# SwiGLU gate and up products in seven half-width block products instead of eight

## The chip, the cores and the metric

The kernel runs on one core of a Trainium2 chip. The metric is device time in microseconds (us), the median of several runs; lower is better. Times of the trace come from one profiled execution. TensorE is called PE, its weight loads PEld, VectorE DVE, ScalarE ACT, GpSimd POOL and SyncE SP.

## The reference, cut to what matters

Four residual layers work on 512 tokens of width 1024, all in float32. Each layer is a token mixer and a SwiGLU feed-forward (FFN); the mixers are attention, a gated MLP, a state-space mixer and attention again. The change is in the FFN, which occurs four times:

```python
FFN_HIDDEN = 2816                                  # 22 tiles of 128 columns, 11 pairs of tiles
def rmsnorm(x, g):
    y = x * lax.rsqrt(jnp.mean(x * x, axis=-1, keepdims=True) + EPS)
    return y * g
def swiglu(h, w_gu, w_down):                       # h: 512 x 1024, w_gu: 1024 x 5632, w_down: 2816 x 1024
    gu = h @ w_gu
    return (jax.nn.silu(gu[..., :FFN_HIDDEN]) * gu[..., FFN_HIDDEN:]) @ w_down
x = x + m                                          # m: the mixer
x = x + swiglu(rmsnorm(x, ffn_norm[i]), ffn_w_gu[i], ffn_w_down[i])
```

## The kernel before, in words

Activations stand feature-major: a tile is 128 features by 512 tokens, so x is eight tiles. Each float32 operand of a product is split into a hi part (rounded to the fp32r type, one pass on PE) and a lo part (the rest); a product is then three matmuls, hi by hi, hi by lo and lo by hi (`mm3`). The stationary operand of a matmul is a 128x128 block of weights, the moving one 512 tokens.

Weights come from memory in `raw` tiles of 1 MB (128 x 2048 numbers), two buffers of them (`RAWB`). A class `Stream` brings them in the order in which they are used. Each raw tile is cut into two pieces of 1024 columns; `to_hi` writes the hi part (`whi`) on ACT or DVE, `to_lo` the lo part (`wlo`) by a subtraction on DVE or POOL. Three pieces may stand ready or in use (`WB`).

An FFN (`ffn`) goes through 12 hidden tiles and then through 10. For every pair of hidden tiles it multiplies the gate columns (`fm`, 48 matmuls of 512 tokens into two PSUM banks), then the up columns in the same way. The gate's bank is scaled by the reciprocal norm (`rstdB`) on DVE, goes through Silu on ACT, and is scaled again on DVE; the up bank is multiplied by it and split into hi and lo. When all pairs of the part are done, `outp` multiplies them with the rows of `w_down` and `residual` adds the bank to x.

The order of work on PE, ACT, DVE and POOL is written out at build time by a class `Order`. It keeps a clock of its own with a cost for each kind of instruction, and chooses by it where an instruction goes that could run on two engines (`pick` for hi parts, `better_g` for lo parts and sums) and when it is issued. Its costs count a DVE instruction with both inputs in SBUF and a POOL instruction as excluding each other. On the chip each engine then goes through its list in that order and waits on semaphores.

Of the kernel before, what the change touches and what calls it, by code (L numbers as in the profile page):

```python
# [17 lines left out]
F32 = mybir.dt.float32  # L21
F32R = mybir.dt.float32r
AF = mybir.ActivationFunctionType
ALU = mybir.AluOpType
# [41 lines left out]
class Parts:  # L66


    def __init__(self):
        self.hi = self.lo = None  # L70
        self.ready = Task()


class Order:
# [230 lines left out]
class Stream:  # L305


    def __init__(self, k):
        self.k, self.o = k, k.o
        self.raws, self.pieces = [], []  # L310
        self.next_raw = self.next_piece = 0
        self.done_raw = 0
        self.slack = 0.0

    def add(self, srcs, cuts, side=False):


        raw = {"srcs": srcs, "left": len(cuts)}
        self.raws.append(raw)
        out = []  # L320
        for c in cuts:
            p = {"raw": raw, "cut": c, "n": len(self.pieces), "task": Task(), "side": side}
            self.pieces.append(p)
            out.append(p)
        return out

    def dma(self, dst, srcs, n):

# [4 lines left out]
        return Task(self.o.book("D", 0.00143 * n) + 2.0)  # L333

    def load(self):
        while self.next_raw < min(len(self.raws), self.done_raw + RAWB):
            r = self.raws[self.next_raw]
            self.next_raw += 1
            a, b = r["srcs"][0].shape[1], sum(q.shape[2] for q in r["srcs"])
            t = self.k.wp.tile([P, 2048], F32, tag="raw", name="raw", bufs=RAWB)  # L340
            r["ap"] = t[:, :a * b].rearrange("p (a b) -> p a b", b=b)
            r["task"] = self.dma(r["ap"], r["srcs"], a * b)

    def first(self):

        r = self.raws[0]
        self.next_raw = 1
        t = self.k.wp.tile([P, 2048], F32, tag="raw", name="raw", bufs=RAWB)
        r["ap"] = t.rearrange("p (a b) -> p a b", b=256)
        for n, p in enumerate(self.pieces[:2]):  # L350
            ks = slice(4 * n, 4 * n + 4)
            p["loaded"] = self.dma(r["ap"][:, ks, :], [q[:, ks, :] for q in r["srcs"]], 1024)
            yield

    def issue(self):
        if self.next_piece >= len(self.pieces):
            return
        p = self.pieces[self.next_piece]
        self.next_piece += 1
        self.load()  # L360
        self.o.spawn(self._split(p))

    def _split(self, p):
        nc, o, r = self.k.nc, self.o, p["raw"]
        yield p.get("loaded") or r["task"]
# [3 lines left out]
        lo = self.k.wp.tile([P, 1024], F32R, tag="wlo", name="wlo", bufs=WB)  # L369
        if p["side"]:  # L370
# [8 lines left out]
        r["left"] -= 1  # L379
        if not r["left"]:  # L380
            self.done_raw += 1
            self.load()
        o.finish(p["task"])

    def release(self, p):

        def later():
            yield self.o.clk
            self.issue()
        self.o.spawn(later())  # L390


class Trunk:
    def __init__(self, ctx, tc, io):
        self.tc, self.nc, self.io = tc, tc.nc, io
        self.o = Order()
        pool = lambda **k: ctx.enter_context(tc.tile_pool(**k))


        self.tiny = pool(name="tiny", bufs=1)  # L400
        self.const = pool(name="const", bufs=1)
# [8 lines left out]
        self.stream = Stream(self)  # L410


    def bank_cond(self, kind="ps", n=1):
# [100 lines left out]
    def setup(self):  # L514
# [13 lines left out]
        with self.tc.tile_pool(name="xin", bufs=1, reuse_waits="tile") as pool:  # L528
# [4 lines left out]
            for q in range(4):  # L533
# [3 lines left out]
                xtok.append(v)  # L537
                if q % 2 == 1:
                    next(first)
            for _ in range(WB):  # L540
                self.stream.issue()
            self.sb_consts(pool)
            o.until(lambda: 4.5)
            ps = self.bank()
# [95 lines left out]
        self.x_ready, self.acc_ready = [Task() for _ in range(KT)], Task()  # L640
        self.last_sq, self.n_sq = None, 0

    def residual(self, d, ps, last, kind, next_sub):

        nc, o = self.nc, self.o
        nc.vector.tensor_tensor(self.xT[d], self.xT[d], ps, op=ALU.add)  # L646
        yield o.V(S)
        self.give(kind)
# [71 lines left out]

        return self.stream.add(srcs, [(0, 4, 0, 256), (4, 8, 0, 256)])

    def fm(self, pieces, evac, kind="ps"):

        yield self.bank_cond(kind, 2)
        banks = [self.bank(kind) for _ in range(2)]
        for n, p in enumerate(pieces):
            for qs, i in self.steps():
# [6 lines left out]
                if k == KT - 1:  # L735
                    self.o.spawn(evac(i, banks[i]))
            self.stream.release(p)

    def steps(self):

# [58 lines left out]
    def outp(self, reg, ys, last, kind="ps"):  # L799

        nk, next_sub = len(ys), self.next_sub
        if last:
# [1 line left out]
        for cg, chunks in enumerate(reg):  # L804
            banks = [None] * 4
            for a, b, pieces in chunks:
                d = -1
                for p in pieces:
                    for i in range((p["cut"][3] - p["cut"][2]) // P):
# [9 lines left out]
                            self.mm3(banks[d], (p["h"][:, k - a, c], p["l"][:, k - a, c]),  # L819
                                     (ys[k].hi, ys[k].lo), k == 0, k == nk - 1)  # L820
                        if b == nk:
                            self.o.spawn(self.residual(cg * 4 + d, banks[d], last, kind, next_sub))
                    self.stream.release(p)


    def reg_ffn(self, l):
        wgu = self.io["ffn_w_gu"][l].rearrange("(k p) f -> p k f", p=P)
        wd = self.io["ffn_w_down"][l].rearrange("(f p) d -> p f d", p=P)
        parts, f0 = [], 0
        for nf in (12, 10):  # L830
            gu = []
            for f in range(f0, f0 + nf, 2):
                gu.append([self.reg_in([wgu[:, :, b + f * P:b + (f + 2) * P]]) for b in (0, HID)])
            parts.append((nf, gu, self.reg_out(wd[:, f0:f0 + nf, :])))
            f0 += nf
        return parts

    def ffn(self, l, parts):
        nc, o = self.nc, self.o
        with self.tc.tile_pool(name=f"ffn{l}", bufs=3, reuse_waits="tile") as pool:  # L840
            self.stats(pool)
            for half, (nf, gu, down) in enumerate(parts):
                ys = []
                for g_pieces, u_pieces in gu:
                    gates, two = [None, None], [Parts(), Parts()]
                    n0 = len(ys)
                    ys += two

                    def gate(i, ps, gates=gates):
                        gates[i] = pool.tile([P, S], F32, tag="g", name="g", bufs=4)  # L850
                        yield self.rstdB_ready
                        nc.vector.tensor_tensor(gates[i], ps, self.rstdB, op=ALU.mult)
                        yield o.V(S)
                        self.give()
                        nc.scalar.activation(gates[i], gates[i], AF.Silu)
                        yield o.A(S, tab="silu")
                        yield self.either(gates[i], gates[i], self.rstdB, ALU.mult, S)

                    tasks = {}

                    def gate_(i, ps, tasks=tasks, gate=gate):
                        tasks[i] = o.spawn(gate(i, ps))
                        return
                        yield

                    def up(i, ps, tasks=tasks, gates=gates, two=two, n0=n0):
                        yield tasks[i]
                        a = pool.tile([P, S], F32, tag="a", name="a")
                        nc.vector.tensor_tensor(a, ps, gates[i], op=ALU.mult)
                        yield o.V(S)  # L870
                        self.give()
                        yield from self.parts(two[i], pool, f"a{n0 + i}", a)
                    o.run(self.fm(g_pieces, gate_))
                    o.run(self.fm(u_pieces, up))
                o.run(self.outp(down, ys, half == 1))


    def reg_gm(self, j):
# [911 lines left out]
```

## Time and profile before

| what | value |
|---|---|
| time, median of 3 runs (lowest to highest) | 2779.15 us (2777.06 to 2781.51) |
| time of the profiled execution | 2776.99 us |
| its span, first to last instruction | 2775.1 us |
| PE busy | 2746.3 us, 99% of the span |
| DVE, ACT, POOL busy | 64%, 33%, 19% |
| mean granted clock of TensorE | 0.999 of full speed |

The busy share of PE is a union of matmuls that overlap as they pass through the array: a matmul of 512 tokens is shown 390 ns long, but the next one starts 227 ns after it. So the price of a matmul is read from the distance of starts, or from a run's time divided by its count, not from its own duration. The same holds in a small way for DVE and ACT, whose instructions overlap their neighbours by about 0.1 us.

### The profile page before, as it was taken

Reading aid. Unit: us, or ns where it says so; the run is one execution under the profiler, and the core shown is the slowest. Engines: PE = TensorE matmul, PEld = TensorE weight load, DVE = VectorE, ACT = ScalarE, POOL = GpSimd, SP = SyncE. Lnnn points to the kernel's source line nnn. Section 1 sums busy time; section 2 is a strip of 40 time slices with the busy share of each in tenths; the row PEclk is TensorE's granted clock in tenths of the full one; section 3 lists DMA queues with packets and bytes.
Section 4 is the critical chain, followed back from the end, with each engine's and each line's share of the span. In section 5 each row is a group of like instructions: output and inputs, shape, how many; then the busy total and the mean of one; then the engine's idle time right before and its main releaser. Section 6 shows DMA issues by size and latency. Waiting matters only on the chain.

```text
span 2775.1 us, 34968 instructions
## 1 busy us (share of the span) xinstructions
PE 2746.3 (99%) x14339; PEld 2357.7 (85%) x14339; DVE 1766.5 (64%) x2505; ACT 928.4 (33%) x1532; POOL 522.3 (19%) x397
## 2 busy tenths in 40 slices
PE   8999999999999999999999999999999999999999
PEld 8998788888888888888898898888889999788887
DVE  7887854555465655455887787754555887865453
ACT  4876410113222211112553353310113786511111
POOL 4665400002011100001311011200004656400000
PEclk9999999999999999999999999999999999999999
DMA  4110232234333222323222222223222111222322
GB/s 138 49 61 31 91 105 93 92 98 125 99 99 95 92 91 93 105 88 97 77 76 76 77 77 77 91 91 104 94 90 94 62 48 53 81 94 91 103 91 80
DMA packets 207967, 240.72 MB, mean 87 GB/s; under 512 B 6448, under 2 KB 170416, under 8 KB 207808
## 3 DMA queue, kind: packets, MB, share of 16 engines
q1 hardware_dynamic: 207552, 238.36, 27.2%
q8 instruction: 112, 1.84, 0.3%
q14 instruction: 47, 0.39, 0.0%
q0 software_dynamic: 160, 0.11, 0.0%
q10 hardware_dynamic: 96, 0.03, 0.0%
HBM read 236.38 MB, written 2.10 MB: 86 GB/s over the span
## 4 chain that ended last, share of the span: by engine, by line
PE 95%; DVE 2%; POOL 1%; issue 1%; ACT 1%; DMA 0%; ACTq 0%; SPq 0%; POOLq 0%; DVEq 0%
PE ps L458 85%; PE z L458 4%; PE c L458 3%; PE t L458 1%; DVE xl L616 1%; PE c L472 1%; PE t L472 0%; DMA ws<-in_gm_w_s 0%; DVE x L646 0%; POOL r L502 0%; POOL wlo L502 0%; ACT whi L479 0%; DVE sp_r L1043 0%; DMA rows<-in_ffn_norm 0%; DVE wlo L500 0%
## 5 line engine op out<-in xcount | busy, mean ns | idle before, releaser
L458 PE MATMUL ps<-xh,whi 128*128 128x512 f32 x1792 | 701.9, 392 | 0.0
L458 PE MATMUL ps<-xl,whi 128*128 128x512 f32 x1792 | 698.6, 390 | 2.7 <-DVE xl L616 2.5
L458 PE MATMUL ps<-xh,wlo 128*128 128x512 f32 x1792 | 697.7, 389 | 0.0
L479 ACT CAST whi<-raw 128x1024 fp32r<-128x1024 f32 (+2 forms) x245 | 239.2, 977 | 933.9 <-PE ps L458 881.3
L500 DVE TENSOR_TENSOR wlo<-raw,whi 128x1024 fp32r<-128x1024 f32 (+2 forms) x371 | 450.5, 1214 | 120.3 <-ACT whi L479 103.3
L481 DVE CAST whi<-raw 128x1024 fp32r<-128x1024 f32 (+1 forms) x224 | 155.2, 693 | 415.6 <-PE ps L458 414.7
L458 PEld LDWEIGHTS ps<-xl,whi 128*128 128x128 f32 x1792 | 336.4, 188 | 77.0 <-DVE xl L616 7.0
L458 PEld LDWEIGHTS ps<-xh,whi 128*128 128x128 f32 x1792 | 336.4, 188 | 70.1 <-issue 1.0
L458 PEld LDWEIGHTS ps<-xh,wlo 128*128 128x128 f32 x1792 | 336.3, 188 | 70.1
L458 PE MATMUL ps<-lo,whi 128*128 128x512 f32 x960 | 373.9, 389 | 1.7 <-POOL lo L502 1.7
L458 PE MATMUL ps<-hi,whi 128*128 128x512 f32 x960 | 375.5, 391 | 0.0
L458 PE MATMUL ps<-hi,wlo 128*128 128x512 f32 x960 | 373.7, 389 | 0.0
L458 PE MATMUL ps<-whi,xh 128*128 128x256 f32 (+1 forms) x1152 | 342.9, 298 | 0.0
L458 PE MATMUL ps<-wlo,xh 128*128 128x256 f32 (+1 forms) x1152 | 339.4, 295 | 0.9 <-DVE wlo L500 0.9
L458 PE MATMUL ps<-whi,xl 128*128 128x256 f32 (+1 forms) x1152 | 339.6, 295 | 0.4 <-DVE xl L616 0.3
L502 POOL TENSOR_TENSOR wlo<-raw,whi 128x1024 fp32r<-128x1024 f32 (+1 forms) x97 | 202.3, 2087 | 301.6 <-ACT whi L479 198.8
L502 POOL TENSOR_TENSOR acc<-acc,sq 128x512 f32<-128x512 f32 x31 | 48.5, 1564 | 1041.8 <-ACT sq L630 1040.9
L458 PEld LDWEIGHTS ps<-wlo,xh 128*128 128x128 f32 x1152 | 220.1, 191 | 7.3 <-DVE wlo L500 1.1
L458 PEld LDWEIGHTS ps<-whi,xh 128*128 128x128 f32 x1152 | 219.9, 191 | 6.7 <-issue 0.4
L458 PEld LDWEIGHTS ps<-whi,xl 128*128 128x128 f32 x1152 | 220.0, 191 | 5.8 <-DVE xl L616 0.8
L458 PEld LDWEIGHTS ps<-lo,whi 128*128 128x128 f32 x960 | 180.3, 188 | 39.0 <-POOL lo L502 2.3
L458 PEld LDWEIGHTS ps<-hi,wlo 128*128 128x128 f32 x960 | 180.2, 188 | 37.8
(227 smaller groups left out, 3374.7 us busy)
## 6 DMA issues: line engine op xcount, KB each, us to landing
raw<-in_ffn_w_gu SPq DMA_DIRECT2D x88, 1024.0 KB, 5.1
raw<-in_ffn_w_down SPq DMA_DIRECT2D x32, 1024.0 KB, 5.1
raw<-in_sb_w_qkv SPq DMA_DIRECT2D x23, 1024.0 KB, 5.1
raw<-in_gm_w_in SPq DMA_DIRECT2D x16, 1024.0 KB, 5.4
raw<-in_ssm_w_in SPq DMA_DIRECT2D x16, 1024.0 KB, 5.5
raw<-in_ffn_w_down SPq DMA_DIRECT2D x16, 768.0 KB, 4.5
raw<-in_gm_w_out SPq DMA_DIRECT2D x8, 1024.0 KB, 5.1
raw<-in_ssm_w_in SPq DMA_DIRECT2D x16, 512.0 KB, 5.3
```

What stands on the lines that cost most here:

```text
L458: self.nc.tensor.matmul(out, lhsT=lhsT, rhs=rhs, start=start, stop=stop, skip_group_check=True)
L472: self.nc.tensor.transpose(out, in_, self.ident[:in_.shape[0], :in_.shape[0]])
L479: self.nc.scalar.copy(h, src)
L481: self.nc.vector.tensor_copy(h, src)
L500: self.nc.vector.tensor_tensor(out, a, b, op=op)
L502: self.nc.gpsimd.tensor_tensor(out, a, b, op=op)
L616: nc.vector.scalar_tensor_tensor(out=self.xl[d], in0=x, scalar=gcol(d), in1=self.xh[d].bitcast(F32), op0=ALU.mult, op1=ALU.subtract)
```

## The change

In each FFN the first two pairs of hidden tiles stay as they were ("plain"). For the other nine pairs, the gate columns (128 features x 8 blocks by 256 columns) and the up columns are each taken as a 2 by 2 matrix of blocks: the two hidden tiles by the even and odd blocks of features. The activations are a 2 by 2 matrix too, even and odd blocks by the two halves of the tokens. A 2 by 2 block product has eight block products; here it is written with seven (Strassen's scheme, in Winograd's form). The four weight blocks A11, A12, A21, A22 and the sums S1 = A21 + A22, S2 = S1 - A11, S3 = A11 - A21, S4 = A12 - S2 give the seven weight factors; `halves_in` makes four sums of the activations once per FFN (`th`, `tl`). One product of a factor is 4 blocks x 3 matmuls = 12 matmuls of 256 tokens (`product`). "Unit" below means the gate or the up columns of one pair: seven products, 84 matmuls. The results are put together in SBUF: three banks' contents are copied out by ACT or DVE (`saved`) and three are added by DVE (`added`), one quarter is read straight from its bank.

Each weight factor is split into hi and lo like a piece (512 numbers per partition each): hi on ACT, lo on DVE or POOL. Five of the seven factors go through a ring of six slots (`whi` and `wlo` now both hold whole factors), the factors A22 and S4, used late, through two slots `wt`. A third raw buffer (`more`) is used in the FFN.

The FFN is cut into parts of 8, 8 and 6 hidden tiles, where it was 12 and 10. That makes three sections of units per FFN: 4 units (after the two plain pairs), 8 units and 6 units, each followed by its rows of `w_down`. In the first two parts the second scaling by `rstdB` goes from the gate to `residual`, which then scales the bank (`rx`) and adds it in a second instruction.

```diff
-        for nf in (12, 10):
+        for nf in (8, 8, 6):
             gu = []
             for f in range(f0, f0 + nf, 2):
-                gu.append([self.reg_in([wgu[:, :, b + f * P:b + (f + 2) * P]]) for b in (0, HID)])
+                cols = [wgu[:, :, b + f * P:b + (f + 2) * P] for b in (0, HID)]
+                gu.append([self.reg_in([c]) if f < 4 else self.reg_fast(c) for c in cols])
...
+    def _sums(self, r):                                        # in Stream: the four weight sums of a raw tile
+        o, fast = self.o, r["fast"]
+        yield r["task"]
+        A = {(i, j): r["ap"][:, j - 1::2, (i - 1) * P:i * P] for i in (1, 2) for j in (1, 2)}
...
+        def put(name, dst, a, b, op):
+            yield self.k.either(dst, a, b, op, 512)
...
+        yield from put("S1", s1, A[2, 1], A[2, 2], ALU.add)
...
+        yield from put("S2", s2, s1, A[1, 1], ALU.subtract)
+        yield from put("S3", A[2, 1], A[1, 1], A[2, 1], ALU.subtract)
+        yield fast["A12"]["task"]
+        yield from put("S4", A[1, 2], A[1, 2], s2, ALU.subtract)
...
+    def _factor(self, p, before, placed, tail=False):          # hi and lo of one factor
...
+        yield self.k.to_hi(h, p["src"], 512)
+        yield self.k.to_lo(l, p["src"], h, 512, self.slack)
...
     def to_hi(self, h, src, n, even=True):
         o = self.o
-        if o.pick(A=0.00083 * n + 0.1, V=(0.00052 if even else 0.00104) * n + 0.07) == "A":
+        late = 0.0 if self.fpool is None else 1.5
+        if o.pick(A=0.00083 * n + 0.1, V=(0.00052 if even else 0.00104) * n + 0.07 + late) == "A":
...
+    def product(self, u, name, bank, start):
+        p = u.p[name]
+        for k in range(4):
+            x, w = self.factor_x(name, k), (p["h"][:, k, :], p["l"][:, k, :])
+            for n, (a, b) in enumerate(((0, 0), (0, 1), (1, 0))):
+                self.nc.tensor.matmul(bank[:, :S // 2], lhsT=w[a], rhs=x[b], start=start and k == 0 and n == 0,
+                                      stop=False, skip_group_check=True)
+                self.o.pe(0.1207)
+        self.stream.release(p)
+
+    def fast(self, units):
...
+        for u in units:
...
+            self.product(u, "A11", u.X, True)
+            u.t = u.make()
+            o.spawn(saved(u.t[0][:, :H], u.X, u.s1))
...
+            self.product(u, "A12", u.Y, True)
+            o.spawn(added(u.t[0][:, :H], u.Y, u.s1, u.c11, True))
+            o.spawn(u.rest())
+            if prev is not None:
+                yield from p4(prev)                            # product A22 of the unit before, into its X
+            yield o.due(u.p["S2"]["task"], u.s1)
+            self.product(u, "S2", u.X, False)
+            o.spawn(saved(u.t[0][:, H:], u.X, u.s2))
+            if prev is not None:
+                yield from p3(prev)                            # product S4 of the unit before, into its Z
...
+            self.product(u, "S1", u.Z, True)
+            yield o.due(u.p["S3"]["task"], u.s2)
+            self.product(u, "S3", u.X, False)
+            o.spawn(saved(u.t[1][:, H:], u.X, u.s3))
+            o.spawn(added(u.t[1][:, H:], u.Z, u.s3, u.c22, False))
+            prev = u
...
-    def residual(self, d, ps, last, kind, next_sub):
+    def residual(self, d, ps, last, kind, next_sub, by):
...
+            t = self.fpool.tile([P, S], F32, tag="a", name="rx", bufs=4)
+            nc.vector.tensor_tensor(t, ps, by, op=ALU.mult)
+            yield o.V(S)
+            self.give(kind)
+            yield self.either(self.xT[d], self.xT[d], t, ALU.add, S)
```

On PE, in the first FFN, where the third pair's gate columns begin, the list of before has these rows (`xh`, `xl` are hi and lo of an activation tile, `whi`, `wlo` those of a weight piece, the last number the tokens):

```order
L458 MATMUL ps<-xh_91,wlo 128x512
L458 MATMUL ps<-xh_84,whi 128x512
L458 MATMUL ps<-xl_92,whi 128x512
L458 MATMUL ps<-xh_84,wlo 128x512
L458 MATMUL ps<-xh_85,whi 128x512
L458 MATMUL ps<-xl_93,whi 128x512
```

The list of the changed kernel at the same place, from the end of product A12 to the begin of product S2 (`wlo` here holds hi and lo of one factor, `whi` those of the next; `th`, `tl` are hi and lo of a sum of activations):

```order
L906 MATMUL ps<-xh_91,wlo 128x256
L906 MATMUL ps<-xl_99,wlo 128x256
L906 MATMUL ps<-xh_91,wlo 128x256
L906 MATMUL ps<-th_3944,whi 128x256
L906 MATMUL ps<-tl_3945,whi 128x256
L906 MATMUL ps<-th_3944,whi 128x256
L906 MATMUL ps<-th_4031,whi 128x256
```

The matmuls are half as wide, and every one has a weight load of its own, as before.

On DVE, at the third pair, the list of before has one gate pair and its neighbours like this:

```order
L852 TENSOR_TENSOR g<-ps,rstdB 128x512
L500 TENSOR_TENSOR wlo<-raw,whi 128x1024
L500 TENSOR_TENSOR g<-g,rstdB 128x512
L481 CAST whi<-raw 128x1024
L500 TENSOR_TENSOR wlo<-raw,whi 128x1024
L869 TENSOR_TENSOR a<-ps,g 128x512
L481 CAST hi<-a 128x512
L500 TENSOR_TENSOR lo<-a,hi 128x512
```

The list of the changed kernel at its first units (`sum`, `raw<-raw`, `raw<-raw,sum` are weight sums, `whi<-raw,whi` and `wlo<-raw,wlo` lo parts of factors):

```order
L603 TENSOR_TENSOR whi<-raw,whi 128x512
L929 TENSOR_TENSOR g<-ps,g 128x256
L603 TENSOR_TENSOR raw<-raw,sum 128x4x128
L603 TENSOR_TENSOR whi<-sum,whi 128x512
L603 TENSOR_TENSOR sum<-raw 128x512
L603 TENSOR_TENSOR wlo<-raw,wlo 128x512
L603 TENSOR_TENSOR sum<-sum,raw 128x512
L929 TENSOR_TENSOR g<-ps,g 128x256
L603 TENSOR_TENSOR raw<-raw 128x4x128
L603 TENSOR_TENSOR g<-g,rstdB 128x256
```

The hi casts are gone from DVE to ACT, the instructions are more and shorter, and most of them read two operands in SBUF. On POOL the list of before has, from the norm of the first FFN on to the begin of the next layer, these rows (`acc` belongs to the next norm, `ws` to the next layer):

```order
L502 TENSOR_TENSOR wlo<-raw,whi 128x1024
L502 TENSOR_TENSOR lo<-a,hi 128x512
L502 TENSOR_TENSOR acc<-acc,sq 128x512 x5
L502 TENSOR_TENSOR wlo<-raw,whi 128x1024
L902 AFFINE_SELECT ws<-ws 128x512 x4
```

The list of the changed kernel, at its first units:

```order
L605 TENSOR_TENSOR whi<-raw,whi 128x512
L605 TENSOR_TENSOR whi<-sum,whi 128x512
L605 TENSOR_TENSOR wt<-raw,wt 128x512
L605 TENSOR_TENSOR sum<-more 128x512
L605 TENSOR_TENSOR more<-more 128x4x128
L605 TENSOR_TENSOR wlo<-sum,wlo 128x512
```

POOL, which had hardly anything to do in an FFN, now has about a third of the sums and lo parts of its sections.

## Rows read from the trace of the kernel before

**Rows 1.** The page: span and busy time of the engines.
```profile
span 2775.1 us, 34968 instructions
PE 2746.3 (99%) x14339; PEld 2357.7 (85%) x14339; DVE 1766.5 (64%) x2505; ACT 928.4 (33%) x1532; POOL 522.3 (19%) x397
```
**Rows 2.** Chain of waits, stretches of FFN 1, 3, 4: start, length, what, matmuls.
```profile
314.40 347.20 PE ps L458 x1532
...
1743.13 371.26 PE ps L458 x1640
...
2415.23 320.18 PE ps L458 x1413
```
**Rows 3.** Engines' busy time in FFN 1 and FFN 4, and the four FFNs' sum.
```profile
322.00:666.00 344.00, 344.00 (x1517) 284.44 (x1518) 183.90 (x229) 55.52 (x71) 14.14 (x8) 1.00 0.30 95
...
2423.00:2769.00 346.00, 346.00 (x1537) 286.03 (x1537) 174.02 (x220) 50.57 (x63) 6.02 (x3) 1.00 0.29 92
sum 1391.00, PE 1391.00 PEld 1150.15 DVE 729.32 ACT 216.95 POOL 42.40; mean PE 347.75 PEld 287.54 DVE 182.33 ACT 54.24 POOL 10.60
```
**Rows 4.** Chain of waits, early runs of 256-wide matmuls (first attention).
```profile
29.02 20.20 PE ps L458 x168
...
50.09 5.75 PE ps L458 x48
```
**Rows 5.** Groups by line and shape: busy, mean ns of one, idle before.
```profile
L458 PE MATMUL ps<-whi,xh 128*128 128x256 f32 x1024 | 292.6, 286 | 0.0
L500 DVE TENSOR_TENSOR lo<-a,hi 128x512 fp32r<-128x512 f32 x86 | 63.0, 733 | 5.5 <-ACT hi L479 2.8
L1338 DVE TENSOR_TENSOR yo<-c,eac 128x256 f32<-128x256 f32 x24 | 8.8, 414 | 0.0
L479 ACT CAST r<-s 128x512 fp32r<-128x512 f32 x76 | 47.0, 620 | 5.8 <-DVE s L1626 4.3
L1620 ACT ACTIVATE s<-z 128x256 f32<-128x256 f32 x32 | 12.2, 382 | 0.0
L502 POOL TENSOR_TENSOR r<-s,r 128x512 fp32r<-128x512 f32 x52 | 69.5, 1337 | 84.7 <-ACT r L479 39.2 <-DVE r L481 32.2 <-PE ps L458 13.1
```
**Rows 6.** Timeline, instructions back to back: DVE, then POOL.
```profile
290.20 2.48 DVE L646 TENSOR_TENSOR x<-x,ps 128x512 f32<-128x512 f32 x4
...
147.10 1.29 POOL L502 TENSOR_TENSOR r<-s,r 128x512 fp32r<-128x512 f32 x1 [5.72 <-DVE r L481]
148.36 1.29 POOL L502 TENSOR_TENSOR wlo<-raw,whi 128x512 fp32r<-128x512 f32 x1
```
**Rows 7.** Timeline of FFN 1, DVE and POOL at the same time.
```profile
335.03 2.40 POOL L502 TENSOR_TENSOR wlo<-raw,whi 128x1024 fp32r<-128x1024 f32 x1 [10.73 <-ACT whi L479]
335.51 2.47 DVE L500 TENSOR_TENSOR lo<-a,hi 128x512 fp32r<-128x512 f32 x1 [1.39 <-ACT hi L479]
337.38 1.74 POOL L502 TENSOR_TENSOR lo<-a,hi 128x512 fp32r<-128x512 f32 x1
337.90 0.68 DVE L852 TENSOR_TENSOR g<-ps,rstdB 128x512 f32<-128x512 f32 x1
```
**Rows 8.** Engines' busy time in the first attention, columns as in rows 3.
```profile
85.00:300.00 215.00, 210.08 (x1421) 194.75 (x1421) 172.47 (x264) 157.06 (x311) 123.16 (x85) 0.98 0.16 53
```
**Rows 9.** The page, DMA issues: KB each, us to landing.
```profile
raw<-in_ffn_w_gu SPq DMA_DIRECT2D x88, 1024.0 KB, 5.1
```

More of the change, by code (lines that the diff above doesn't have):

```diff
@@ L325, in add, with add_fast @@
         return out
+    def add_fast(self, src):
+        raw = {"srcs": [src], "left": 7, "tag": ("more", "raw", "raw")[self.n_fast % 3], "loaded": Task(), "fast": {}}
+        self.n_fast += 1
+        self.raws.append(raw)
+        for name in ("A11", "A12", "S2", "S1", "S3", "A22", "S4"):
+            p = raw["fast"][name] = {"raw": raw, "task": Task(), "name": name, "slots": 1, "ready": Task()}
+            (self.tails if name in ("A22", "S4") else self.pieces).append(p)
+        return raw["fast"]
     def dma(self, dst, srcs, n):
@@ new lines, in issue, with _place, _done @@
+        while self.next_tail < len(self.tails) and self.tail_credit and self.k.fpool is not None:
+            p = self.tails[self.next_tail]
+            self.next_tail += 1
+            self.tail_credit -= 1
+            self.o.spawn(self._factor(p, *self._place(1), True))
+    def _place(self, ring):
+        before, self.placed[ring] = self.placed[ring], Task()
+        return before, self.placed[ring]
+    def _done(self, p):
+        r = p["raw"]
+        r["left"] -= 1
+        if not r["left"]:
+            self.flying[r["tag"]] -= 1
+            self.load()
+        self.o.finish(p["task"])
@@ L364, in _split @@
+    def _split(self, p, before, placed):
         nc, o, r = self.k.nc, self.o, p["raw"]
-        yield p.get("loaded") or r["task"]
+        yield r["loaded"]
+        yield [p.get("half") or r["task"], before]
         a0, a1, b0, b1 = p["cut"]
@@ L378, in _split @@
         p["h"], p["l"] = h, l
[L379 to L383, printed above, removed]
+        self._done(p)
     def release(self, p):
@@ L388, in later @@
             yield self.o.clk
+            if p.get("name") in ("A22", "S4"):
+                self.tail_credit += 1
+            else:
+                self.credit += p["slots"]
             self.issue()
@@ L539, in setup @@
                     next(first)
-            for _ in range(WB):
-                self.stream.issue()
+            self.stream.issue()
             self.sb_consts(pool)
@@ L797, in reg_out, with outp @@
                  for a, b in cuts] for c in (0, 512)]
-    def outp(self, reg, ys, last, kind="ps"):
+    def outp(self, reg, ys, last, kind="ps", between=(), by=None):
         nk, next_sub = len(ys), self.next_sub
@@ L821, in outp @@
                         if b == nk:
-                            self.o.spawn(self.residual(cg * 4 + d, banks[d], last, kind, next_sub))
+                            self.o.spawn(self.residual(cg * 4 + d, banks[d], last, kind, next_sub, by))
                     self.stream.release(p)
+                    yield from between
+                    between = ()
     def reg_ffn(self, l):
@@ L839, in ffn @@
         nc, o = self.nc, self.o
+        H = S // 2
+        gcol = self.gain(("ffn", l, l))
         with self.tc.tile_pool(name=f"ffn{l}", bufs=3, reuse_waits="tile") as pool:
+            self.fpool = pool
             self.stats(pool)
[L842 to L853, printed above, removed]
-                        self.give()
[L855 to L862, printed above, removed]
@@ L863, in gate_ @@
                         return
                         yield
[L866 to L873, printed above, removed]
@@ L874, in ffn, with gated @@
-                    o.run(self.fm(u_pieces, up))
-                o.run(self.outp(down, ys, half == 1))
+                    return gen
+                def gated(i):
+                    yield from silu(g.t[i], n)
+                    o.finish(done[i])
+                r = self.rstdB_ready
+                g.quarter = quarter(g, lambda: self.rstdB, r)
+                g.rest = rest(g, lambda i: self.rstdB, [r, r], gated)
+                u = Unit(u_pieces)
+                u.make = lambda: [new_a(), new_a()]
@@ new lines, in units, with gu_steps @@
+                u.quarter = quarter(u, lambda: g.t[1], done[1])
+                u.rest = rest(u, lambda i: g.t[i], done, lambda i: self.parts(two[i], pool, f"a{n0 + i}", u.t[i]))
+                return [g, u]
+            for n, (nf, gu, down) in enumerate(parts):
+                ys, todo, left = [], [], []
+                for g_pieces, u_pieces in gu:
+                    two = [Parts(), Parts()]
+                    if n == 0 and len(ys) < 4:
+                        plain(g_pieces, u_pieces, two, n, len(ys))
+                    else:
+                        todo += units(g_pieces, u_pieces, two, n, len(ys))
+                    ys += two
+                def gu_steps():
+                    left.append((yield from self.fast(todo)))
+                o.run(gu_steps())
+                last = n == len(parts) - 1
+                o.run(self.outp(down, ys, last, between=left[0], by=None if last else self.rstdB))
@@ L878, in reg_gm @@
+        self.fpool = None
     def reg_gm(self, j):
```

223 lines of the change are left out of this document (204 added, 19 removed).

## The prediction

> **What bounds the kernel now.** I read the page first: PE is busy for 2746.3 of 2775.1 us, no other engine above 64% [rows 1]. That alone says little, since matmuls overlap in the records, so the chain of waits came next. In the FFNs it is a single run of PE: 347.20 us with 1532 matmuls without a step between, and the like in the other FFNs [rows 2]. The table by stretches gives the neighbours: over the four FFNs' 1391 us PE is busy all the time at the full clock (1.00), DVE for 729 us (52%), ACT for 217, POOL for 42 [rows 3]. So an FFN costs exactly what its matmuls cost, and whatever takes PE time out is gained as long as the other three keep PE fed. The question is whether they do, as DVE, ACT and POOL get the work for it.
>
> **PE's part.** A 512-wide matmul costs 347.20 / 1532 = 0.2266 us [rows 2]. The trace also has long runs of 256-wide ones of the same kind (fp32r, a full 128x128 weight load for each, 1024 per group [rows 5]): 20.20 / 168 = 0.1202 us and 5.75 / 48 = 0.1198 us [rows 4]. So half the width costs 53%, not 50%: some 13 ns of each matmul do not shrink. A unit (gate or up columns of a pair) was 48 matmuls of 512: 48 x 0.2266 = 10.88 us. It becomes 84 of 256: 84 x 0.120 = 10.08 us. The gain is 0.80 us a unit, 7% where seven products for eight would be 12.5%. There are 4 FFNs x 9 pairs x 2 = 72 units: 72 x 0.80 = 57.4 us (55.9 with the one price, 58.7 with the other). The products with the rows of w_down, and the plain pairs, keep their matmuls.
>
> By the Trainium skill, "TensorE: Matmul & The Clock Gate", Back-to-back issue gap, starts are N/2.4 + 2.5 ns apart, 216 ns and 109 ns. With that the sum would be 3456 x 0.216 - 6048 x 0.109 = 87 us, an estimate from that page. The rows have both widths and give 227 and 120, so the sum goes by the rows.
>
> **What is added beside PE.** I take the 8-unit section of an FFN, 80.6 us of PE, and count in the order what stands on the engines between its first and last 256-wide product. DVE: 62 instructions of 512 columns (or a little less) with both inputs in SBUF, 31 that read a PSUM bank, mostly 256 wide. POOL: 37 of 512. ACT: 66 from SBUF, mostly casts of 512, and 24 copies of 256 from PSUM.
> ACT: 66 x 0.62 + 24 x 0.38 = 50 us of 80.6 [rows 5]. It has room; hi parts come in time, and the casts that left DVE fit there.
> DVE: a row of 512 reads 0.69 to 0.73 us, but four in a row take 2.48 us, with 0.68 for the last: (2.48 - 0.68) / 3 = 0.60 us each [rows 5, 6]. The same for POOL: the second starts 1.26 us after the first [rows 6], 1.34 is the mean of the records [rows 5]. By themselves: DVE 62 x 0.60 + 31 x 0.41 = 50 us, POOL 37 x 1.26 = 47 us. Each fits into 80.6 us.
> They do not run freely beside each other, though. The POOL instruction at 335.03 lasts to 337.43; a DVE subtraction of two SBUF operands issued at 335.51 shows 2.47 us and ends 0.55 us after POOL's end, so it stood still for POOL. The next POOL instruction, at 337.38, needs 1.74 us in place of 1.29, as it waits for that DVE one. The DVE instruction at 337.90 reads a bank, and takes its usual 0.68 us beside POOL [rows 7]. So I add the two kinds that exclude each other: 62 x 0.60 + 37 x 1.26 = 83.8 us against 80.6 of PE. Those on PSUM banks go beside POOL. In the 6-unit section (46 and 31, 60.5 us of PE) it is 66.7; in the 4-unit one (35 and 11) 34.9 against 40.3.
> The Trainium skill, "SBUF — State Buffer", Who interferes with whom, has it as an exclusive lock of a port pair for the whole instruction, for a DVE instruction with two SBUF inputs against a POOL one that reads SBUF, and none for one with at most one SBUF input; the trace agrees with 2.47 and 0.68 us. It is the rule that speaks against this change.
>
> So the two sections run over by 3.2 and 6.2 us. What hides this is the stock: in the order a factor's lo part mostly stands six products ahead of its use, 72 x 0.120 = 8.6 us, and the stock is filled anew while w_down's products run (192 or 144 matmuls of 512, 43.5 or 32.6 us, with 25 DVE instructions and few on POOL). If the instructions cost their recorded lengths instead, the excess is 62 x 0.69 + 37 x 1.34 - 80.6 = 11.8 us and, likewise, 12.8 us, so 3.2 + 4.2 us of PE waits in an FFN, 30 us in four. Bounds of this unknown are 0 and 30 us. I take 4 us, near the lower end, since the pitch of neighbours is what a saturated engine shows; 1 us for each FFN at the end of its 6-unit section, where the order leaves least (a lo part stands 1.8 to 3.7 us ahead).
> A new wait is that of product S2 on the copy of its bank: within the first unit of a section only product A12 (1.44 us) lies between, and ACT's copy of 0.38 us stands behind at most a cast of 0.62 us. With semaphores that is about even: 0 to 0.3 us, 12 sections, I take 2 us. From the second unit on two products lie between, 2.9 us. Behind a late DVE addition, on DVE, stand lo parts that have the same stock.
> Hidden altogether: the sums of the activations (on DVE 12 instructions of 256 columns and 8 of 512 per FFN, some 11 us) beside the plain pairs' 43.5 us of PE, where DVE was half idle; 24 residuals in place of 16 and their second instruction, beside w_down's products; the DMAs, the same bytes, with 5.1 us to land [rows 9] against 10 us a unit and three buffers. Without that cover each would cost what it takes: the residuals, for one, 0.6 to 0.7 us apiece.
>
> **Sum.** Against the profiled execution, 2776.99 us (1.9 over its span): 2776.99 - 57.4 + 4 + 2 = 2725.6. That execution lies 2.2 us under the median of the runs, so 2727.8, called 2728.
>
> **Rivals.**
> Vector-limited sections, still a gain. For it: DVE and POOL together are over PE's time in two of three sections. Against: the stock, and the first attention, where DVE is at 172 and POOL at 123 of 215 us, more than the 70% and 60% here, while PE stays busy for 210 [rows 8]. By the recorded lengths 30 us come back: 2779 - 57 + 30 = 2752; up to 2774.
> Slower. The mechanism: DVE and POOL in single file, those on PSUM banks too, since DVE goes through its list in order and an addition that waits for its product holds up the lo parts behind it. Per unit (62 x 0.69 + 37 x 1.34 + 31 x 0.41) / 8 = 13.1 us against 10.08: 3.06 x 72 = 220 us, less 8.6 us of stock in each of 12 sections = 103: 117 back for 57 gained, 2839 us. It decides from 10.08 + (57 + 103) / 72 = 12.3 us per unit on. For it: the count above is 10.5 us with nothing else. Against: rows 7 (the bank-reader at full speed) and rows 8.
> No change: the waits come to about the 57 us, 2779. It needs 12.3 us a unit just so.
> PE's narrow matmuls cheaper than the early runs show: starts 109 and 216 ns apart would give 2779 - 87 + 6 = 2698. Against: every 256-wide run of the trace.
>
> **How the numbers follow.** Forecast (2718 to 2740) 0.70; vector-limited with a gain 0.14; no change 0.06; slower 0.08; cheaper matmuls 0.02. So faster 0.70 + 0.14 + 0.02 = 0.86, same 0.06, slower 0.08, with 0.2% (5.6 us) as about what a measurement of this kernel can tell from no change. The range goes from 2717 (58.7 us gained, no wait, 3 us of spread of the runs) to 2752 (30 us of waits).
>
> **What would show it.** Right: the 256-wide products start 0.120 us apart in stretches without waits; an FFN's PE run gets 14 us shorter; DVE at about 70% and POOL at 60% in the 8-unit sections; PE's idle time in an FFN a microsecond or two, at the last units of the 6-unit section. Wrong: PE waits for lo parts (DVE or POOL) in the middle of the 8-unit sections, or for the copies of ACT in every unit; a start distance other than 0.120; DVE instructions of 512 with two SBUF inputs at a mean well over 0.9 us.

## The result, and the profile after

The changed kernel takes 2729.53 us (2728.78 to 2734.62, 4 runs); the kernel before took 2778.57 us (2777.06 to 2781.51, 4 runs) beside it. The ratio is 0.9823, with a 95% interval of 0.9808 to 0.9839: 49 us faster. The prediction was 2728, with a range from 2717 to 2752. The profiled execution took 2728.8 us, its span is 48.0 us shorter than before.

The page, span and busy time of each engine, as in [rows 1]:

```profile
span 2727.1 us, 42302 instructions
PE 2692.4 (99%) x16931; PEld 2435.6 (89%) x16931; DVE 2149.2 (79%) x2994; ACT 1337.1 (49%) x2366; POOL 1070.0 (39%) x762
```

PE stays the engine that sets the time. It has 2592 matmuls more and is busy 54 us less, while POOL's work has doubled. Long pieces of the chain of waits in FFN 1 and 2 (start, length, what, matmuls; columns as in [rows 2]):

```profile
354.17 34.82 PE ps L906 x288
397.33 38.11 PE ps L560 x168
435.44 41.77 PE ps L906 x348
...
979.95 37.43 PE ps L906 x312
```

A 256-wide matmul costs 41.77 / 348 = 0.1200 us, a 512-wide one 38.11 / 168 = 0.2268 us. These are the two prices of the sum.

Busy time in the three sections of FFN 1 (4, 8 and 6 units), columns as in [rows 3]:

```profile
350.60:397.00 46.40, 45.84 (x360) 44.69 (x359) 40.43 (x55) 24.25 (x47) 16.78 (x11) 1.00 0.34 114
435.30:522.00 86.70, 86.49 (x697) 85.13 (x696) 79.91 (x95) 47.98 (x92) 56.50 (x38) 1.00 0.33 106
560.20:626.00 65.80, 64.71 (x523) 63.78 (x522) 60.61 (x72) 35.48 (x69) 46.41 (x33) 1.00 0.25 85
```

In the 8-unit section, the second row, DVE (third pair of numbers) is busy for 79.91 of 86.7 us (92%) and POOL (the fifth) for 56.50 (65%). Yet PE idles for little. What it waits for is in the view of waits (us in total, times, longest), the entries of the 256-wide products, of PE and of its weight loads:

```profile
PE ps L906 <- DVE a L929: 4.4, 4, 1.1
...
PE ps L906 <- ACT g L920: 1.1, 2, 0.6
```
```profile
PEld ps L906 <- DVE a L929: 5.2, 4, 1.3
...
PEld ps L906 <- DVE g L929: 2.5, 8, 0.4
```

L920 is the copy of a bank by ACT, for which product S2 waits. L929 is the addition of a bank to what is saved in SBUF. Product S4 goes into the bank Z after product S1's content has been added out of it (the quarter C22), so it waits for this addition. The timeline of the 6-unit section of FFN 1 shows why that is late:

```profile
598.55 1.75 POOL L605 TENSOR_TENSOR g<-g,rstdB 128x512 f32<-128x512 f32 x1
...
599.07 1.78 DVE L603 TENSOR_TENSOR raw<-raw,sum 128x512 f32<-128x512 f32 x1
...
600.26 1.74 POOL L605 TENSOR_TENSOR wlo<-raw,wlo 128x512 fp32r<-128x512 f32 x1
...
600.77 1.78 DVE L603 TENSOR_TENSOR whi<-raw,whi 128x512 fp32r<-128x512 f32 x1
...
601.96 1.74 POOL L605 TENSOR_TENSOR sum<-raw 128x512 f32<-128x512 f32 x1
...
602.47 1.77 DVE L603 TENSOR_TENSOR g<-g,rstdB 128x512 f32<-128x512 f32 x1
...
603.65 1.73 POOL L605 TENSOR_TENSOR wt<-raw,wt 128x512 fp32r<-128x512 f32 x1
604.17 0.41 DVE L929 TENSOR_TENSOR a<-ps,a 128x256 f32<-128x256 f32 x1
...
604.63 0.39 PE L906 MATMUL ps<-xh,wt 128*128 128x256 f32 x1 [1.09 <-DVE a L929]
```

DVE and POOL take strict turns: one instruction of each in 1.70 us (600.77 - 599.07, and 602.47 - 600.77). A DVE instruction of 512 columns with both inputs in SBUF shows 1.78 us in place of the 0.7 of [rows 5]. The addition itself takes 0.41 us; it stands behind three such instructions, and PE waits for it.

Against the pitches of 0.120 and 0.2267 us I counted what PE loses from start to start within each section:

| section | FFN 1 and 4 | FFN 2 and 3 | where |
|---|---|---|---|
| 4 units | 0.83 | 0.01 | 0.7 at product S2 of the first unit |
| 8 units | 0.73 | 0.73 | 0.5 at two products S4 |
| 6 units | 1.36 | 1.36 | 1.25 at one product S4 |

The columns stand for two FFNs each, so these are 10.0 us in all twelve sections. So 57.4 - 10.0 = 47.4 us should have gone from the span, and 48.0 went.

### The profile page after: what moved, and what is told of

It is laid out like the page before. It is cut to its first block, busy times and chain, and to the rows that moved or that the text cites. A ratio compares the mean times of both kernels' runs of the same rounds, so it can differ in the third digit from the quotient of the medians.

```text
span 2727.1 us, 42302 instructions
## 1 busy us (share of the span) xinstructions
PE 2692.4 (99%) x16931; PEld 2435.6 (89%) x16931; DVE 2149.2 (79%) x2994; ACT 1337.1 (49%) x2366; POOL 1070.0 (39%) x762
## 4 chain that ended last, share of the span: by engine, by line
PE 89%; DVE 7%; issue 1%; POOL 1%; DMA 0%; ACT 0%; ACTq 0%; SPq 0%; DVEq 0%; POOLq 0%
PE ps L560 58%; PE ps L906 21%; PE z L560 5%; PE c L560 3%; PE t L560 1%; DVE wlo L603 1%; DVE whi L603 1%; DVE raw L603 1%; DVE xl L718 1%; PE c L574 1%; DVE wt L603 1%; PE t L574 0%; DVE g L603 0%; DVE x L749 0%; DMA ws<-in_gm_w_s 0%
## 5 line engine op out<-in xcount | busy, mean ns | idle before, releaser
L605 POOL TENSOR_TENSOR wlo<-raw,whi 128x1024 fp32r<-128x1024 f32 (+2 forms) x108 | 226.3, 2097 | 319.4 <-ACT whi L582 198.9
L603 DVE TENSOR_TENSOR wlo<-raw,whi 128x1024 fp32r<-128x1024 f32 (+2 forms) x216 | 271.3, 1257 | 94.6 <-ACT whi L582 88.8
L560 PE MATMUL ps<-xh,whi 128*128 128x512 f32 x640 | 254.0, 397 | 0.0
L560 PE MATMUL ps<-xl,whi 128*128 128x512 f32 x640 | 250.6, 392 | 2.7 <-DVE xl L718 2.4
L560 PE MATMUL ps<-xh,wlo 128*128 128x512 f32 x640 | 249.7, 390 | 0.0
L560 PEld LDWEIGHTS ps<-hi,whi 128*128 128x128 f32 x960 | 180.4, 188 | 36.7 <-ACT hi L582 0.7
L906 PE MATMUL ps<-th,whi 128*128 128x256 f32 x864 | 173.3, 284 | 1.1 <-ACT g L920 1.1
L906 PE MATMUL ps<-th,wlo 128*128 128x256 f32 x864 | 173.1, 283 | 0.0
L749 DVE TENSOR_TENSOR x<-x,ps 128x512 f32<-128x512 f32 x168 | 112.7, 682 | 63.7 <-PE ps L560 63.2
L560 PEld LDWEIGHTS ps<-xl,whi 128*128 128x128 f32 x640 | 120.3, 188 | 31.9 <-DVE xl L718 6.9
```

What stands on the lines that cost most here:

```text
L560: self.nc.tensor.matmul(out, lhsT=lhsT, rhs=rhs, start=start, stop=stop, skip_group_check=True)
L603: self.nc.vector.tensor_tensor(out, a, b, op=op)
L605: self.nc.gpsimd.tensor_tensor(out, a, b, op=op)
L906: self.nc.tensor.matmul(bank[:, :S // 2], lhsT=w[a], rhs=x[b], start=start and k == 0 and n == 0, stop=False, skip_group_check=True)
```

## The experiments

Every time below stands beside runs of the kernel before on the same chip (2777 to 2780 us).

**Vector work on DVE alone.** The theory (A): PE's 10 us come from the turns that DVE and POOL take, and not from DVE's amount of work. All sums and lo parts of the FFN go to DVE:

```diff
-        if not o.better_g(n, slack):
+        if self.fpool is not None or not o.better_g(n, slack):
```

> In the FFNs every sum and lo part goes to DVE, none to POOL; all else as in the changed kernel (2729.5 us). Theory A (PE waits about 10 us in all, because DVE additions stand behind DVE instructions that wait for POOL): without POOL an 8-unit section asks (62 + 37) x 0.60 + 31 x 0.33 = 70 us of DVE against 80.6 of PE, nothing excludes anything, PE's waits shrink: 2720 to 2726. Rival B (DVE needs POOL's help; its instructions cost their recorded lengths): 99 x 0.69 + 31 x 0.41 = 81 us, at the limit, waits grow: 2732 to 2760.

Measured: 2715.09 us (2714.44 to 2720.16), ratio 0.9772 (0.9756 to 0.9787). The sections lose 0.01 us each. The window of its 8-unit section in FFN 1:

```profile
431.80:517.90 86.10, 86.10 (x698) 85.14 (x697) 75.16 (x136) 49.02 (x91) 0.00 (x0) 1.00 0.34 111
```

DVE does 136 instructions in place of 95 and is busy for less time, 75.16 in place of 79.91 us, since none of it is spent standing behind POOL. Its rows follow each other at 0.60 us again:

```profile
592.39 0.69 DVE L603 TENSOR_TENSOR wt<-more,wt 128x512 fp32r<-128x512 f32 x1
...
592.99 0.69 DVE L603 TENSOR_TENSOR sum<-raw 128x512 f32<-128x512 f32 x1
...
593.60 0.69 DVE L603 TENSOR_TENSOR whi<-raw,whi 128x512 fp32r<-128x512 f32 x1
```

Theory A is borne out; the time is even below its range, which counted on the ten microseconds alone. The span is 13.6 us shorter than that of the changed kernel: 9.9 from the sections, 2.7 ahead of the first section (where in the changed kernel the norm's additions on POOL stretch DVE's lo parts of x in the same way: 2.28 us for one in place of 0.74), 1.0 elsewhere. This version beats both kernels.

**Vector work on POOL alone.** The opposite, for the price of POOL:

```diff
-            yield self.k.either(dst, a, b, op, 512)
+            self.k.nc.gpsimd.tensor_tensor(dst, a, b, op=op)
+            yield self.o.G(512)
...
-        yield self.k.to_lo(l, p["src"], h, 512, self.slack)
+        self.k.nc.gpsimd.tensor_tensor(l, p["src"], h.bitcast(F32), op=ALU.subtract)
+        yield self.o.G(512)
```

> All weight sums and all lo parts of factors go to POOL, 11 instructions per unit; all else as in the changed kernel. The stock theory: POOL needs 11 x 1.26 = 13.9 us per unit against 10.08 of PE, sections of 8, 6 and 4 units lose 21.6, 14.3 and 6.6 us after 8.6 us of stock, four times: 2730 + 170 = 2900. If each POOL instruction stands for a DVE one too (1.70 us): 18.7 us per unit, 3240. Without a stock (every unit pays in full, 1.26): 72 x 3.8 = 274, 3000. If POOL and DVE did not exclude each other and POOL ran at 1.04: 11.4 us a unit, 2740.

Measured: 2967.95 us (2964.38 to 2972.76), ratio 1.0685 (1.0669 to 1.0701). The 8-unit section of FFN 1:

```profile
445.60:560.00 114.40, 96.84 (x697) 92.44 (x696) 47.18 (x61) 46.12 (x87) 108.66 (x80) 0.93 0.25 84
```

This is above the stock theory's 2900 us and below the 3000 of the one without a stock. POOL is busy for 108.66 of 114.40 us with 80 instructions, 1.36 us each. That lies between its own pitch and that of turns with DVE, and both are to be seen in its timeline:

```profile
472.60 1.28 POOL L457 TENSOR_TENSOR wt<-more,wt 128x512 fp32r<-128x512 f32 x1
473.83 1.29 POOL L457 TENSOR_TENSOR whi<-more,whi 128x512 fp32r<-128x512 f32 x1
...
474.65 1.03 DVE L605 TENSOR_TENSOR a<-a,g 128x512 f32<-128x512 f32 x1
...
475.08 1.76 POOL L457 TENSOR_TENSOR wlo<-raw,wlo 128x512 fp32r<-128x512 f32 x1
...
476.79 1.74 POOL L457 TENSOR_TENSOR whi<-raw,whi 128x512 fp32r<-128x512 f32 x1
```

With nobody beside it the next instruction starts after 1.24 us; where DVE comes between, after 1.7. This section loses 28.4 us, where the theory with the stock of lo parts had 21.6 at 1.26 us apiece. At 1.36 it has 8 x (11 x 1.36 - 10.08) - 8.6 = 30.4 us, and 62 us for the three sections of an FFN; all twelve lost 248, which is 62 each. The stock is there: PE's first wait in this section comes 22 us after its start. The granted clock is 0.93 in this section, in which PE is idle for 17.6 us; some 8 of the 28.4 us are starts further apart, the rest waits. Whether the clock cost anything beyond POOL's pace isn't shown.

**No sums.** Factors S1 to S4 taken as plain blocks, so the four weight sums of a unit are left out and the output is another; all products and lo parts stay:

```diff
-        yield from put("S1", s1, A[2, 1], A[2, 2], ALU.add)
...
-        yield from put("S4", A[1, 2], A[1, 2], s2, ALU.subtract)
...
+        for name, b in (("S1", (2, 1)), ("S2", (2, 2)), ("S3", (2, 1)), ("S4", (1, 2))):
+            fast[name]["src"] = A[b]
+            o.finish(fast[name]["ready"])
```

> Leaves out the four weight sums of each unit: factors S1 to S4 are taken as plain blocks, so four vector instructions of eleven per unit are gone and the products are not the FFN's. The matmuls are the same. Theory A: only about 10 us of PE waits are there to win: 2718 to 2724. Rival B (the sections are limited by vector work throughout): clearly under 2715.

Measured: 2723.33 us (2722.9 to 2723.87), ratio 0.9798 (0.9784 to 0.9812). The sections lose nothing. The 8-unit section of FFN 1:

```profile
433.00:520.00 87.00, 87.00 (x702) 85.89 (x701) 62.93 (x108) 49.27 (x93) 0.00 (x0) 1.00 0.34 110
```

The time is in theory A's range. But with less to do the planner gives POOL next to nothing, so this run, too, has no turns, and it doesn't price the sums by themselves. The version with DVE alone is 8 us quicker than this one though it does all the sums. The difference lies outside the sections: 2.0 us ahead of the first section of FFN 1, 5.0 in the third mixer, 1.6 ahead of the first section of FFN 4. That in the mixer is PE's granted clock (the third number from the end), first this run, then that with DVE alone:

```profile
1650.00:1733.00 83.00, 79.86 (x408) 68.86 (x407) 59.97 (x99) 35.79 (x56) 18.20 (x14) 0.94 0.20 64
```
```profile
1650.00:1733.00 83.00, 79.85 (x430) 68.47 (x430) 64.83 (x108) 38.63 (x60) 17.30 (x13) 1.00 0.27 89
```

Sixty matmuls behind a wait of 2.0 us for POOL take 14.9 us here and 10.0 us there, and 10.0 in the changed kernel.

**Product S4 later.** If the wait is that of S4 on the addition, S4 of the unit before, issued after product S1 in place of before it, gives the addition 1.4 us more:

```diff
-            if prev is not None:
-                yield from p3(prev)                            # product S4 of the unit before, into its Z
             yield self.both(o.due(u.p["S1"]["task"]), self.bank_cond())
             u.Z = self.bank()
             self.product(u, "S1", u.Z, True)
+            if prev is not None:
+                yield from p3(prev)
```

> Product S4 of the unit before comes after product S1 in place of before it, 1.44 us later; nothing else is changed on purpose. Theory A (what PE waits for is the addition of quarter C22 on DVE, which must be done before S4 writes into its bank): the waits before S4 go (1.25 us in the 6-unit sections, two of 0.2 to 0.3 in the 8-unit ones, four FFNs): 7 us less, 2721 to 2725. Rival C (lo parts come late and the S4 wait only shows it first): the wait moves to another product, 2728 to 2731.

Measured: 2731.48 us (2729.98 to 2736.55), ratio 0.983 (0.9814 to 0.9846): no gain, half a microsecond above rival C's range. The waits on L929 are gone from the list and others stand there, nearly all at the rows of w_down at the end of the 6-unit section and behind it:

```profile
PE ps L560 <- ACT hi L582: 4.3, 4, 1.2
PE ps L560 <- DVE wlo L603: 3.3, 5, 0.9
```

The 8-unit sections lose 0.01 us in place of 0.73, the 6-unit ones 0.92 in place of 1.36, and the rest is lost right behind. So the addition was what PE waited for, but taking that wait away gained nothing: another chain ends just behind it. In FFN 1 it goes from DVE's lo parts of w_down (two in 3.93 us) over the load that follows them (landed at 624.50 us), ACT's hi part, the next lo part on DVE (2.03 us beside POOL) and the activations' hi part to PE at 630.61. That DVE is late as a whole fits this, though it idles for 2.3 us in that chain, for the load; the planner's list changed with the edit, too.

**Narrow matmuls alone.** The kernel before, with each 512-wide matmul of the gate and up columns of the last nine pairs cut into two of 256:

```diff
-                    self.mm3(banks[i], (p["h"][:, q, c], p["l"][:, q, c]), (self.xh[k], self.xl[k]),
-                             k == 0, k == KT - 1)
...
+                    for t in (slice(0, 256), slice(256, 512)):
+                        self.mm3(banks[i][:, t], (p["h"][:, q, c], p["l"][:, q, c]),
+                                 (self.xh[k][:, t], self.xl[k][:, t]), k == 0 and t.start == 0, k == KT - 1)
```

> The kernel before, with the gate and up matmuls of all pairs but the first two of each FFN cut in two along the tokens: 6912 matmuls of 256 for 3456 of 512, same sums, same vector work. By the rows (0.120 and 0.2266 us): 6912 x 0.120 - 783.1 = 46 us more, 2825. By the price N/2.4 + 2.5 ns (109 and 216 ns): 6912 x 0.109 - 3456 x 0.216 = 7 us more, 2786. If a second matmul with the same weights were cheaper, less than 46.

Measured: 2826.53 us (2822.28 to 2828.91), before 2777.21, ratio 1.0173 (1.0158 to 1.0188). The starts on PE:

```profile
399.94 0.28 PE L458 MATMUL ps<-xh,wlo 128*128 128x256 f32 x1
400.06 0.28 PE L458 MATMUL ps<-xh,whi 128*128 128x256 f32 x1
400.18 0.28 PE L458 MATMUL ps<-xl,whi 128*128 128x256 f32 x1
```

0.120 us apart; 3456 x (2 x 0.1200 - 0.2266) = 46 us are expected by the rows, 49 came. The profiled execution, 2828.78 us, lost 4.9 of it to the clock in the third mixer again (0.94 from 1700 to 1783 us; 1.00 in the kernel before); without these it lies 47 us above that of the kernel before. So the smaller gain of 7% in place of 12.5% is the price of 256-wide matmuls by itself.

**Parts of 8, 8 and 6 alone.** All pairs plain, with the new parts and the scaling moved to the residual (the hi parts choose between ACT and DVE as before):

```diff
-                gu.append([self.reg_in([c]) if f < 4 else self.reg_fast(c) for c in cols])
+                gu.append([self.reg_in([c]) for c in cols])
...
-                    if n == 0 and len(ys) < 4:
+                    if True:
```

> The kernel before with the parts of 8, 8 and 6 hidden tiles and the scaling of the residual by the reciprocal norm in the first two, every pair plain, no seven-product units. Theory A: the extra residual instructions lie beside PE: within 3 us of before, 2776 to 2782. Rival: the third part costs or gives something of its own, more than 5 us either way.

Measured: 2778.53 us (2775.64 to 2782.88, 10 runs), ratio 1.0 (0.999 to 1.0009). Theory A holds: these edits cost nothing. Its chain has FFN 1 as one run again, 0.2266 us per matmul:

```profile
311.59 347.16 PE ps L560 x1532
```

**One plain pair.** The second pair in seven products too (8 more units, 6.4 us of PE to gain), which takes away half the cover for the sums of the activations:

```diff
-                gu.append([self.reg_in([c]) if f < 4 else self.reg_fast(c) for c in cols])
+                gu.append([self.reg_in([c]) if f < 2 else self.reg_fast(c) for c in cols])
...
-                    if n == 0 and len(ys) < 4:
+                    if n == 0 and len(ys) < 2:
```

> Only the first pair of each FFN stays plain, the second is done in seven products too: 8 units more. Theory A: 8 x 0.80 = 6.4 us less PE time, 2721 to 2725, if the sums of the activations are ready 21.8 us of PE earlier. Rival D (the sums of the activations or the first factors come too late): PE waits at the begin of the first section by as much or more, 2727 to 2745.

Measured: 2792.03 us (2788.8 to 2792.61), ratio 1.0043 (1.003 to 1.0056), slower than before and far above both theories; rival D had the place right and the size too small. The waits of PE:

```profile
PE ps L906 <- ACT g L920: 32.4, 4, 8.9
PE ps L560 <- DVE diag L807: 20.3, 3, 7.5
```

The wait for `diag` is one for the reciprocal norm (`rstd`): at the start of an FFN it stands on POOL behind a row of the new work, each instruction stretched to 1.7 us:

```profile
329.33 1.71 POOL L605 TENSOR_TENSOR sum<-sum,raw 128x512 f32<-128x512 f32 x1
...
331.00 1.70 POOL L605 TENSOR_TENSOR wt<-more,wt 128x512 fp32r<-128x512 f32 x1
...
332.66 1.46 POOL L802 TENSOR_TENSOR rstd<-ms,mhalf 128x4 f32<-128x4 f32 x1
```

PE's granted clock falls, too: it is 0.81 from 315 to 345 us, in which PE is busy for 19 of 30 us.

**One plain pair, DVE alone.** The two edits together ask whether this was the turns again, or the cover:

> This is the version with all sums and lo parts of the FFN on VectorE, and with the second pair of hidden tiles of each FFN in seven products too (one pair stays plain). Theory A (what held PE up was VectorE and GpSimd taking turns, and VectorE alone keeps up): where one plain pair with both engines lost 11.4 to 12.5 us in each FFN's first section, here nothing is stretched; the gain is at most 8 units x 0.80 = 6.4 us below the version with VectorE alone (2715.09), so 2709 to 2715. Theory B (one plain pair is too short a cover for the sums at an FFN's start, on whichever engine they run): PE waits in each first section again, 6 to 12 us times 4, and the time is 2735 to 2765.

Measured: 2758.77 us (2757.36 to 2759.95), ratio 0.9928 (0.9911 to 0.9944). Theory B. The first section of an FFN loses 10.1 to 10.5 us, the others 0.01. The chain of waits ahead of it, in part:

```profile
329.46 0.60 DVE tl L603
330.06 1.20 DVE g L1105 x2
331.26 0.60 DVE tl L603
331.86 1.25 DVE a L1114 x2
333.11 0.39 DVE t L870
333.50 0.60 DVE lo L603
...
339.01 0.62 ACT th L582
339.63 0.28 ACT g L920
339.91 0.04 issue
339.96 5.09 PE ps L906 x28
```

Here nothing is stretched. DVE works nearly without a pause at 0.60 and 0.40 us apiece on the sums of the activations (`t`, `tl`), with the plain pair's banks and lo parts (`g`, `a`, `lo`) among them, and the copy that product S2 waits for (`g L920`) stands in ACT's list behind the casts of these sums. The waits of PE, as in the run before:

```profile
PE ps L906 <- ACT g L920: 33.1, 4, 8.4
...
PE ps L560 <- DVE diag L807: 4.5, 4, 1.8
```

Taking the turns away is worth 33 us against the run before. The copy is waited for as long as there, so that wait is the cover; of the 10.1 to 10.5 us of a first section it is 8.3 to 8.5, and most of the rest is PE behind it at a granted clock of 0.66 (339.90 to 345 us). Against the version with DVE alone, 5 us more go to the clock in the third mixer (0.94 there in this run, too) and 4.5 to `diag`.

**Both, and S4 later.** This is the run before with the edit of "Product S4 later" added:

> As the run with VectorE alone and one plain pair, and product S4 with its additions issued after product S1 too. Theory A (waits are gone once VectorE works alone, so the place of S4 matters no more): equal to that run within 3 us. Theory B (PE waits at the start of the section): the bank additions come later in VectorE's list, behind the sums that the next product needs, so the sums are ready earlier and 4 to 10 us come back against that run.

Measured: 2759.38 us (2759.24 to 2760.19), ratio 0.9932 (0.9917 to 0.9947), equal to the run before. Theory A's number holds: without turns the place of S4 doesn't matter, and it doesn't help the sums of the activations.

## Why the prediction was right

**PE's part** was right in both prices, 0.1200 and 0.2268 us, and in the 57.4 us. The run with narrow matmuls confirms it without anything else. The formula N/2.4 + 2.5 ns of the Trainium skill, "TensorE: Matmul & The Clock Gate", Back-to-back issue gap, would have given 87 us, an estimate; that section calls it the gap of an isolated matmul, which the prediction left out, and no run here shows its 109 ns between the starts of these matmuls.

**What is hidden altogether** was right: the parts and the residuals cost 0 in a run of their own. For the activations' sums the run with DVE alone and one plain pair shows that they need their cover: with half of it PE waits 8.3 to 8.5 us in each FFN. Their price without any cover, put at 11 us, no run shows.

**The waits** were mis-sized: 4 + 2 us in the sum, 10.0 measured. Of these, the wait of S2 on the copy, put at 2 us for twelve sections, came to 1.4 us, in two sections only. The end of the 6-unit sections, put at 1 us each, came to 1.25, though at two thirds of the section and not at its end. What was missing is the 8-unit section, 0.7 us in each FFN, and small remains. With 10.0 the sum is 2776.99 - 57.4 + 10.0 = 2729.6; the profiled execution took 2728.8. That 2728 came so near to the median is in part luck: the sum itself, 2725.6, is 3.2 us under the profiled execution, and the 2.2 us added for the median hide half of that, since the changed kernel's median lies only 0.7 us above its profiled execution.

**Their cause** was named wrongly, and that the forecast held even so is luck as well. For the 6-unit sections I expected lo parts to run out. PE waits for a bank addition that stands in DVE's list behind work with POOL in between. That is near to the mechanism that I had put under the rival "slower", DVE's list in its fixed order, but the other way round: there an addition held up lo parts, here lo parts and sums hold up an addition. It costs 4 x (0.73 + 1.36) = 8.4 us, not 117, because additions and two-input work don't stand in single file: [rows 7] had shown the bank-reader at full speed, and the 0.41 us of the addition beside POOL confirms it.

**The excluded time** was overstated. I added 0.60 + 1.26 = 1.86 us for a DVE and a POOL instruction; in turns the pair takes 1.70. The 8-unit section is then 37 x 1.70 + 25 x 0.60 = 77.9 us, within PE's 80.6, and not 83.8. The Trainium skill, "SBUF — State Buffer", Who interferes with whom, says that a DVE instruction with two SBUF inputs contends with a POOL one that reads SBUF, and one with at most one such input does not. It holds in this trace: 1.78 us for a DVE instruction with two SBUF inputs, 0.41 for the one on a bank beside the same POOL work.

**The signs** were partly ill chosen. POOL's share (65%) came near the 60%, but DVE is at 92% and not 70%, as its records include the time behind POOL. For the same reason the mean of DVE's two-input instructions is over 0.9 us, which I had called a sign of being wrong: the group of one of them in the changed kernel (busy, mean ns):

```profile
L603 DVE TENSOR_TENSOR whi<-sum,whi 128x512 fp32r<-128x512 f32 x54 | 60.1, 1113 | 0.0
```

It reads 1113 ns while PE loses only 10 us in twelve sections. A mean duration on a busy engine doesn't tell whether the engine is late; the waits of PE do. PE does wait in the middle of the 8-unit sections, which I had called a sign of being wrong, though for additions and not for lo parts.

**What I didn't ask:** whether POOL helps at all. Each POOL instruction saves DVE 0.60 us and makes the DVE instruction beside it 1.1 us longer (1.70 - 0.60). The sum 62 x 0.60 + 37 x 0.60 + 31 x 0.41 = 72 us for DVE alone, below PE's 80.6, could have been worked out from the same rows; 75.16 us were measured.

## What to carry to other kernels

Before work is shared between two engines that exclude each other, add up what the quicker one would need alone: if that fits under the bound, the share on the slower one can be a loss, here 14 us (2729.5 to 2715.1). Price narrow matmuls by the distance of their starts in the same kernel, since saved columns are not saved time. Where PE waits for a short instruction, look at what stands ahead of it in its engine's list; moving the waiting product alone gained nothing here.

## What the runs showed of the hardware

DVE with two SBUF inputs and POOL alternate one by one when both have work: 1.70 us for a pair of 512 columns, against 0.60 and 1.24 us alone. DVE's reads of a bank pass beside it in 0.41 us.

After PE's idle time the granted clock was lower: 0.81 over a stretch of 30 us in which PE idled for 11 (one plain pair), and 0.93 over 114 us in which it idled for 17.6 (POOL alone), against 1.00 in the same sections of the changed kernel. 1.00 is the level of 2.4 GHz, so part of these stretches ran at 1.2 GHz. With one plain pair and DVE alone some 1.6 us of each first section's loss are this (10.1 to 10.5 us lost, of which 8.3 to 8.5 in the wait ahead).

The same idle time need not have the same price. In the third mixer every version's PE waits 2.0 us for POOL (`xde`). Behind it the granted clock stayed at 1.00 in the profiled executions of the kernel before, the changed kernel and the one with DVE alone, and was 0.53 over 11 us (1698 to 1709 us) in that without sums; the same sixty matmuls took 10.0 and 14.9 us. What decides it stays open. So a difference of 5 us between two versions is read only with a look at their clocks.
